# Expert selection cut into four parts and gathers called inside it, in a two-block transformer kernel

## The chip, the cores and the metric

The kernel runs on one core of a Trainium2 chip. The metric is the time of one launch on the device in microseconds; the median of three runs stands for a kernel. The engines are TensorE (PE: matmuls, with its weight loads as PEld), VectorE (DVE), ScalarE (ACT), GpSimd (POOL) and SyncE (SP). DMAs are issued from the queues of SyncE, GpSimd and ScalarE and share 16 DMA engines.

## The reference

Two transformer blocks over 256 tokens of width 1024 in float32. The first has a state-space mixer, chunked attention and a gated feed-forward layer. The second has two kinds of attention and, instead of a feed-forward layer, a mixture of very many tiny experts, which is where the change lies:

```python
q = (ht @ w_pq).reshape(T, 8, 2, 128)                    # 8 heads, two halves
sub = einsum('thpc,hpnc->thpn', q, peer_keys)            # 128 scores per head and half
s_top, i_top = top_k(sub, 16)
cand_s = s_top[:, :, 0, :, None] + s_top[:, :, 1, None, :]   # 16 x 16 pairs
best_s, pos = top_k(cand_s.reshape(T, 8, 256), 16)       # 16 of 16384 experts per head
gate = softmax(best_s)
act = gelu(einsum('cd,ckd->ck', x, peer_u[expert]))      # 128 experts per token
out = einsum('ck,ckd->cd', gate * act, peer_v[expert])
```

`peer_u` and `peer_v` have 16384 rows of 1024 each. The output is a final norm of the sum.

## The kernel before

Weights are stored as float32 tiles of 128 x 1024 (512 KB). Most matmuls use a split: ScalarE copies a tile to a high part (`whi`, L226), VectorE or, for tiles named in `POOL_LO` or flagged "P" in `specs`, GpSimd subtracts it to get the low part (`wlo`, L231), and TensorE multiplies three combinations. The order in which each engine runs its instructions is made at build time by a planner that follows the program's order where several are ready; `behind` and `chain` add a fixed order by hand. `chain` ties an instruction behind the last one tied on the same engine, as long as `self.tail` is a dictionary.

The expert layer (`peer`) works in stages. (1) Four `w_pq` tiles and, in `route`, twelve more make the queries; `scores` multiplies them with the keys. The results reach SBUF in banks of four of the sixteen head halves (`subs`). (2) `topk` selects on VectorE, first for tokens 0 to 127 (`tt` = 0), then for the others: 16 calls of `topk16` on 128 scores, three sums of candidates, 8 calls of `topk16` on 80 candidates, softmax weights with one exponential on ScalarE (L1406), and index arithmetic with one-hot products (L1434 to L1442). (3) For the first 96 tokens (`TS`) `slots` writes expert numbers and weights into `slot` with six small DMAs of GpSimd's queue (L1497); `sparse` then gathers the rows of `peer_u` with 96 indirect DMAs of 128 rows each (L1504, 512 KB), each followed by a product with accumulation on VectorE (L1509). After all 96 come 96 gathers of `peer_v`, each followed by a sum into `sacc` (L1524). Five `ug` buffers hold gathers. (4) For the other 160 tokens all 16384 experts are computed in 128 blocks: `u_chunk` for the first 44 (`U0`, L1614) and `u_mul` for the other 84 (L1631). Each block is one `peer_u` tile from SyncE's queue, 8 matmuls of TensorE (16 instructions in the trace), and a GELU of ScalarE. SyncE's tiles run ahead by 13 buffers. (5) In the second of these loops `gate_batch` makes, for 8 tokens per 4 blocks, one-hot matrices on VectorE and ScalarE, a matmul on TensorE (L1568), and the products with the gates (L1579 on ScalarE, L1581 on VectorE). (6) The last loop takes 128 blocks of `peer_v` (L1710) on TensorE for the 160 tokens, while the remaining gathers go on. Then come the output norm and the stores.

The calls `next(sparse)` say where in the program's order a gather and its product stand: in the first loop beside blocks from 26 (`S0`) on except each sixth, in the second beside 70 of 84 blocks, in the last loop beside five of six, the rest behind it. `pick` transposes the selection of each `tt` on TensorE behind block 40.

Of the kernel before, what the change touches and what calls it, by code (L numbers as in the profile page):

```python
# [21 lines left out]
D = 1024  # L22
# [110 lines left out]
class Kernel:  # L133
# [4 lines left out]
    def specs(self):  # L138
# [25 lines left out]
        for i in range(4):  # L164
            add(io["w_pq"], (i,), "LP")
        add(io["w_pq"], range(4, 16))
# [1166 lines left out]
    def topk16(self, vals, idx, src, work):  # L1333
        V = self.nc.vector
        V.max(vals[:, 0:8], src)
        V.max_index(idx[:, 0:8], vals[:, 0:8], src)
        V.match_replace(work, vals[:, 0:8], src, LOWEST)
        V.max(vals[:, 8:16], work)
        V.max_index(idx[:, 8:16], vals[:, 8:16], work)
# [34 lines left out]
    def topk(self, R, K, subs):  # L1374
        nc, V, A, G = self.nc, self.nc.vector, self.nc.scalar, self.nc.gpsimd
# [4 lines left out]
        V.tensor_copy(self.iota2, iota[:, :, None].to_broadcast([128, 128, 2]))  # L1380
        it16 = K.tile([128, 16, 16], FP16, name="it16")
        V.tensor_copy(it16, iota[:, 0:16, None].to_broadcast([128, 16, 16]))
        self.picked = []
        for tt in range(2):
            sub = subs[tt]
            vals = K.tile([128, 16, 16], F32, name="vals", bufs=2)
            idx = K.tile([128, 16, 16], U32, name="idx", bufs=2)
            for j in range(16):
                w = K.tile([128, 128], F32, name="work", bufs=2)
                self.topk16(vals[:, j], idx[:, j], sub[:, j], w)  # L1390
            cand = K.tile([128, 8, 80], F32, name="cand")
            v4 = vals.rearrange("p (h s) a -> p h s a", s=2)
            v1, v2 = v4[:, :, 0], v4[:, :, 1]
            V.tensor_tensor(cand[:, :, 0:16], v2, v1[:, :, 0:1].to_broadcast([128, 8, 16]), OP.add)
            V.tensor_tensor(cand[:, :, 16:72].rearrange("p h (a b) -> p h a b", a=7),
                            v1[:, :, 1:8, None].to_broadcast([128, 8, 7, 8]),
                            v2[:, :, None, 0:8].to_broadcast([128, 8, 7, 8]), OP.add)
            V.tensor_tensor(cand[:, :, 72:80], v1[:, :, 8:16], v2[:, :, 0:1].to_broadcast([128, 8, 8]), OP.add)
            best = K.tile([128, 8, 16], F32, name="best")
            pos = K.tile([128, 8, 16], U32, name="pos")  # L1400
            for hd in range(8):
                w = K.tile([128, 80], F32, name="work2", bufs=2)
                self.topk16(best[:, hd], pos[:, hd], cand[:, hd], w)
            e = K.tile([128, 8, 16], F32, name="gexp", bufs=2)
            V.tensor_tensor(e, best, best[:, :, 0:1].to_broadcast([128, 8, 16]), OP.subtract)
            A.activation(e, e, AF.Exp)  # L1406
            s = K.tile([128, 8], F32, name="gsum")
            V.tensor_reduce(s, e, op=OP.add, axis=AX.X)
            V.reciprocal(s, s)
            V.tensor_tensor(e, e, s[:, :, None].to_broadcast([128, 8, 16]), OP.mult)  # L1410
            id2 = K.tile([128, 2, 8, 16, 2], FP16, name="id2")
            for s_ in range(2):
                V.tensor_copy(id2[:, s_].rearrange("p h a t -> p h a t"),
                              idx.rearrange("p (h s) a -> p h s a", s=2)[:, :, s_, :, None].to_broadcast([128, 8, 16, 2]))
            sel = []
            ui = K.tile([128, 2, 128], U32, name="ui")
            uf = K.tile([128, 2, 128], F32, name="uf")
# [5 lines left out]
            ab = K.tile([128, 2, 128], F32, name="ab")  # L1423
            ab16 = K.tile([128, 2, 128], FP16, name="ab16")
            m9 = K.tile([128, 128], F32, name="m9")
# [5 lines left out]
            V.tensor_tensor(ab16[:, 1], ab[:, 1], m9, OP.subtract)  # L1431
            for s_ in range(2):
                eq = K.tile([128, 8, 16, 16], FP16, name="eq", bufs=2)
# [363 lines left out]
```

## Time and profile before

| | us |
|---|---|
| three runs: median (lowest to highest) | 1302.26 (1298.88 to 1309.69) |
| profiled execution, its own time | 1310.38 |
| its span | 1308.6 |
| TensorE busy | 1236.8 (95%) |
| VectorE busy | 896.3 (68%) |
| ScalarE busy | 494.9 (38%) |
| GpSimd busy | 464.0 (35%) |

The profile is of one execution. Times count from the start of the span; about 2 us lie outside it. The expert layer takes the second half: queries and scores up to about 690 us, the first 44 blocks to 788, the other 84 to 990, the last loop to 1292. A matmul's busy time is modelled, so a loop is best timed by the starts of its first and last instructions. "Idle before" is the time that an engine stood still ahead of an instruction, with what ended it.

### The profile page before, as it was taken

How to read it: one execution, taken by the hardware profiler on the slowest of the kernel's cores; microseconds unless marked ns; L12 is line 12 of the kernel's file. 1: busy time of each engine (PE TensorE's matmuls, PEld its weight loads, DVE VectorE, ACT ScalarE, POOL GpSimd, SP SyncE). 2: the span in 40 equal slices, each digit the busy share in tenths (PEclk: the TensorE clock that was granted, in tenths of full speed). 3: DMA queues.
4: the chain of work that ended last, by engine and by line, in shares of the span. 5: the costliest groups of instructions: out<-in, count | busy, mean ns of one | idle time of the engine just before them, and what ended most of it. 6: DMA issues, size and time to landing. Idle time of an engine off the chain costs nothing.

```text
span 1308.6 us, 22647 instructions
## 1 busy us (share of the span) xinstructions
PE 1236.8 (95%) x8650; PEld 1156.7 (88%) x8650; DVE 896.3 (68%) x1787; ACT 494.9 (38%) x1053; POOL 464.0 (35%) x400
## 2 busy tenths in 40 slices
PE   6798989998999999999899999999999999999996
PEld 5687868988979988998799999999999999888896
DVE  8996765899667888548788945777775455454433
ACT  5335655666556845645532214444440000000001
POOL 5941020665105645202300433444444333333310
PEclk9897889999999988999899999999999999999998
DMA  5322355888744737346678799999999999999991
GB/s 196 106 81 77 105 197 176 305 313 319 256 144 166 246 115 240 98 145 208 211 235 307 277 410 407 396 397 401 400 398 401 409 409 409 409 409 409 409 406 49
DMA packets 103116, 361.50 MB, mean 276 GB/s; under 512 B 15136, under 2 KB 15328, under 8 KB 102624
## 3 DMA queue, kind: packets, MB, share of 16 engines
q1 hardware_dynamic: 71904, 251.28, 52.9%
q0 software_dynamic: 30816, 108.26, 21.6%
q8 instruction: 68, 1.11, 0.3%
q10 hardware_dynamic: 288, 0.52, 0.1%
q14 instruction: 40, 0.33, 0.1%
HBM read 356.22 MB, written 2.12 MB: 274 GB/s over the span
## 4 chain that ended last, share of the span: by engine, by line
PE 51%; DMA 22%; DVE 17%; issue 4%; ACT 2%; POOL 2%; SPq 0%; DVEq 0%; POOLq 0%; ACTq 0%
DMA raw<-peer_v 17%; PE m L1631 14%; PE m L272 13%; PE acc L1710 6%; PE m L1614 4%; PE acc L858 4%; DVE wlo L231 4%; PE acc L1105 3%; DMA adaw<-w_ada 2%; PE acc L873 1%; PE g L1568 1%; POOL adaacc L410 1%; DVE adaacc L407 1%; POOL adaacc L412 1%; DMA bias<-bias 1%
## 5 line engine op out<-in xcount | busy, mean ns | idle before, releaser
L1710 PE MATMUL acc<-act,raw 128*128 128x160 f32 x2048 | 294.4, 302 | 8.3 <-DMA raw<-peer_v 1.8
L1710 PEld LDWEIGHTS acc<-act,raw 128*128 128x128 f32 x2048 | 279.8, 190 | 22.8 <-DMA raw<-peer_v 22.8
L231 DVE TENSOR_TENSOR wlo<-raw,whi 128x1024 fp32r<-128x1024 f32 x150 | 232.0, 1558 | 63.8 <-ACT whi L226 60.9
L226 ACT ACTIVATE whi<-raw 128x1024 fp32r<-128x1024 f32 x166 | 174.0, 1055 | 134.8 <-PE m L272 58.1
L1524 DVE SCALAR_TENSOR_TENSOR sacc<-ug,sw,sacc 128x1024 f32<-128x1024 f32 x94 | 120.8, 1285 | 122.3 <-DMA ug<-peer_v,slot 122.3
L1631 PE MATMUL m<-hN,raw 128*128 128x160 f32 x1344 | 187.0, 300 | 0.0
L1631 PEld LDWEIGHTS m<-hN,raw 128*128 128x128 f32 x1344 | 183.2, 190 | 0.0
L1504 POOL DMA_INDIRECT ug<-u_rows,slot x96 | 120.7, 1258 | 149.6 <-DVE act L1639 97.1
L1504 POOL DMA_INDIRECT ug<-peer_v,slot x96 | 90.5, 943 | 156.6 <-DVE sacc L1524 142.9
L1509 DVE SCALAR_TENSOR_TENSOR ug<-ug,hrow 128x1024 f32<-128x1024 f32 x96 | 116.9, 1218 | 26.9 <-DMA ug<-u_rows,slot 26.9
L272 PE MATMUL m<-h_hi,whi 128*128 128x256 f32 x768 | 117.1, 291 | 4.3 <-ACT h_hi L916 3.0
L272 PE MATMUL m<-h_hi,wlo 128*128 128x256 f32 x768 | 113.0, 286 | 5.4 <-DVE wlo L231 4.8
L272 PE MATMUL m<-h_lo,whi 128*128 128x256 f32 x768 | 116.1, 290 | 2.0 <-DVE h_lo L917 2.0
L272 PEld LDWEIGHTS m<-h_hi,whi 128*128 128x128 f32 x768 | 105.5, 196 | 8.8 <-ACT h_hi L916 3.5
L272 PEld LDWEIGHTS m<-h_hi,wlo 128*128 128x128 f32 x768 | 101.1, 192 | 7.7 <-DVE wlo L231 5.6
L272 PEld LDWEIGHTS m<-h_lo,whi 128*128 128x128 f32 x768 | 104.6, 197 | 3.3 <-DVE h_lo L917 2.4
L1718 ACT ACTIVATE fT<-acc,gt 128x160 f32<-128x160 f32 x4 | 1.6, 393 | 274.2 <-DVE fT L1720 274.0
L1614 PE MATMUL m<-hN,raw 128*128 128x160 f32 x704 | 98.2, 302 | 2.6 <-ACT act L1624 2.6
L1614 PEld LDWEIGHTS m<-hN,raw 128*128 128x128 f32 x704 | 97.5, 193 | 2.8 <-ACT act L1624 2.8
L410 POOL TENSOR_TENSOR adaacc<-adaacc,adaw 128x1024 f32<-128x1024 f32 x24 | 66.0, 2749 | 49.4 <-ACT adaw L409 48.9
L231 POOL TENSOR_TENSOR wlo<-raw,whi 128x1024 fp32r<-128x1024 f32 x16 | 39.4, 2473 | 50.3 <-ACT whi L226 44.6
L1636 ACT ACTIVATE ut<-m 128x8 f32<-128x8 f32 (+19 forms) x80 | 19.2, 240 | 99.9 <-PE m L1631 60.5
(526 smaller groups left out, 1811.9 us busy)
## 6 DMA issues: line engine op xcount, KB each, us to landing
raw<-peer_u SPq DMA_DIRECT2D x128, 512.0 KB
raw<-peer_v SPq DMA_DIRECT2D x128, 512.0 KB
raw<-w_in SPq DMA_DIRECT2D x62, 512.0 KB
adaw<-w_ada SPq DMA_DIRECT2D x48, 512.0 KB
raw<-w_gu SPq DMA_DIRECT2D x44, 512.0 KB
raw<-w_down SPq DMA_DIRECT2D x22, 512.0 KB
raw<-w_out SPq DMA_DIRECT2D x16, 512.0 KB
raw<-w_pq SPq DMA_DIRECT2D x16, 512.0 KB
```

Source lines behind the costliest of these rows:

```text
L226: i = self.nc.scalar.activation(hi, t, AF.Copy)
L231: i = e.tensor_tensor(lo, t, hi.bitcast(F32), OP.subtract)
L272: self.nc.tensor.matmul(out, w(k), x(k), start=start and c == 0, stop=stop and c == last)
L410: G.tensor_tensor(accs[1], accs[1], w, OP.add)
L858: self.nc.tensor.matmul(acc[2 * tt + n], a[:, k, tt * 128:tt * 128 + 128], w[:, 512 * n:512 * n + 512], start=first and (tt, n) not in see ...
L1105: self.nc.tensor.matmul(out, a[:, 2 * c + kk, tt * 128:tt * 128 + 128], w[:, 512 * kk:512 * kk + 512], start=c + i + kk == 0, stop=c == 3 ...
L1504: G.indirect_dma_start(t, None, rows, bass.IndirectOffsetOnAxis(self.slot[:, 0, s:s + 1].bitcast(U32), 0))
L1509: i = V.scalar_tensor_tensor(t, t, 1.0, self.hrow[g], op0=OP.mult, op1=OP.mult, accum_out=self.sdot[:, s:s + 1])
L1524: self.last = V.scalar_tensor_tensor(self.sacc[g], t, w, self.sacc[g], op0=OP.mult, op1=OP.add)
L1614: m = nc.tensor.matmul(ps, w[:, 128 * k:128 * k + 128], hN[:, k], start=k == 0, stop=k == 7)
L1631: D(nc.tensor.matmul(ps[:, 0:N], w[:, 128 * k:128 * k + 128], hN[:, k], start=k == 0, stop=k == 7))
L1710: nc.tensor.matmul(part(d), w[:, 128 * d:128 * d + 128], at(i), start=i == 0 and d % 2 == 0, stop=i == 127, skip_group_check=True)
```

## The change

- `specs`: the first four `w_pq` tiles lose the flag "P" (their low parts go from GpSimd to VectorE); tiles 8 to 15 get it (eight low parts go to GpSimd).
- `topk` becomes a generator that yields after each small piece. It works in four parts, by `tt` and half of the heads (`hf`): `first` makes the first-stage selection of some head halves, `second` the rest for four heads. All tiles of `second` are half as wide, and so there are four exponentials. The sum and the division of the softmax move behind the one-hot products. `slots` is called twice, each time for 64 of the 128 experts of a token, and issues six DMAs each time.
- Every VectorE instruction of the selection is tied (`Tied`) in the program's order; `self.tail` is a dictionary from here on, so that the products of gathered rows are tied in the same order.
- Once the first part is done, a gather is called at every third yield from yield 31 on (`EA`, `EV`): 13 of 68 yields. In the first loop they begin at block 32 instead of 26. In the second loop they stand beside three blocks of four and some more, until all 96 are done (`done`).
- `sparse` takes the `u` gathers in the order in which the halves of `slot` are written.
- In the second loop the end of a gate batch comes behind the gather and the late product of its block instead of ahead of them.

```diff
@@ specs
         for i in range(4):
-            add(io["w_pq"], (i,), "LP")
-        add(io["w_pq"], range(4, 16))
+            add(io["w_pq"], (i,), "L")
+        for i in range(4, 16):
+            add(io["w_pq"], (i,), "P" if i >= 8 else "")
@@ topk
+        class Tied:
+            def __getattr__(self, name):
+                f = getattr(nc.vector, name)
+                return lambda *a, **k: outer.chain(f(*a, **k))
+        V = Tied()
...
+        def first(tt, hf, js):
+            if (tt, hf) not in top:
+                top[tt, hf] = [K.tile([128, 8, 16], d, name=n, bufs=3) for n, d in (("vals", F32), ("idx", U32))]
+            vals, idx = top[tt, hf]
+            for j in js:
                 w = K.tile([128, 128], F32, name="work", bufs=2)
-                self.topk16(vals[:, j], idx[:, j], sub[:, j], w)
+                self.topk16(vals[:, j], idx[:, j], subs[tt][:, 8 * hf + j], w, V)
+                yield
+        def second(tt, hf):
...
+            yield
+            for hd in range(4):
                 w = K.tile([128, 80], F32, name="work2", bufs=2)
-                self.topk16(best[:, hd], pos[:, hd], cand[:, hd], w)
+                self.topk16(best[:, hd], pos[:, hd], cand[:, hd], w, V)
+                yield
+            x = K.tile([128, 4, 16], F32, name="gx", bufs=2)
+            V.tensor_tensor(x, best, best[:, :, 0:1].to_broadcast([128, 4, 16]), OP.subtract)
+            A.activation(x, x, AF.Exp)
...
+            s = K.tile([128, 4], F32, name="gsum")
+            V.tensor_reduce(s, x, op=OP.add, axis=AX.X)
+            V.reciprocal(s, s)
+            V.tensor_tensor(e, x, s[:, :, None].to_broadcast([128, 4, 16]), OP.mult)
             if tt == 0:
-                with self.tc.high_priority():
-                    self.slots(e, *sel)
+                self.slots(hf, V, e, *sel)
+            yield
+        yield from first(0, 0, range(0, 4))
+        yield from first(1, 0, range(0, 4))
+        yield from first(0, 0, range(4, 8))
+        yield from second(0, 0)
+        self.ready = True
+        yield from first(0, 1, range(0, 8))
+        yield from second(0, 1)
+        yield from first(1, 0, range(4, 8))
+        yield from second(1, 0)
+        yield from first(1, 1, range(0, 8))
+        yield from second(1, 1)
@@ slots
         for t0, n in self.TG:
+            h = n // 2
             for q in range(128 // n):
-                self.dq.dma_start(self.slot[n * q:n * q + n, :, t0:t0 + n], ids[t0:t0 + n, :, n * q:n * q + n])
+                self.dq.dma_start(self.slot[n * q:n * q + n, :, t0 + h * hf:t0 + h * hf + h],
+                                  ids[t0:t0 + n, :, h * q:h * q + h])
@@ sparse
-        for g, s in slots:
+        early = [(g, t0 + n // 2 * hf + s) for hf in range(2) for g, (t0, n) in enumerate(self.TG) for s in range(n // 2)]
+        for g, s in early:
@@ constants
-    S0 = 26
+    S0 = 32
+    EA = 31
+    EV = 3
@@ peer
-            sparse, self.tail = self.sparse(), None
+            sparse, self.tail = self.sparse(), {}
...
-                    self.topk(R, K, subs)
+                    self.ready, given = False, 0
+                    for n, _ in enumerate(self.topk(R, K, subs)):
+                        if self.ready and n >= self.EA and (n - self.EA) % self.EV == 0:
+                            next(sparse)
+                            given += 1
...
                     if c % 4 == 0:
-                        if live is not None:
-                            next(live, None)
-                            n += 8
+                        fin = live
                         live = self.gate_batch(O, pg, act, TS + 2 * c, lambda: cur[0]) if 2 * c < N else None
                     if live is not None:
                         mm = next(live)
-                    if c % 4 or c % 12 == 0:
+                    if (c % 4 != 1 or c % 8 == 1) and self.done < TS:
                         next(sparse)
                     late()
+                    if c % 4 == 0 and fin is not None:
+                        next(fin, None)
+                        n += 8
                     late = u_mul(i, n, U)
```

## Rows read from the trace of the kernel before

**Rows 1.** DMA queues, 700 to 740 us, all queues together

```profile
DMA packets 2680, 9.70 MB, mean 243 GB/s; under 512 B 375, under 2 KB 439, under 8 KB 2548
```

**Rows 2.** Table of stretches: start:end, length, busy by engine, PEclk, DMA share, GB/s

```profile
800.00:850.00 50.00, 50.00 (x414) 49.81 (x413) 34.59 (x81) 23.78 (x91) 21.62 (x17) 1.00 1.01 399
1100.00:1200.00 100.00, 94.61 (x630) 86.20 (x629) 49.14 (x39) 0.00 (x0) 36.65 (x39) 1.00 1.03 409
```

**Rows 3.** DMA queues, 1100 to 1200 us: packets, MB, share of 16 engines

```profile
q1 hardware_dynamic: 5629, 20.50, 51.2%
q0 software_dynamic: 5567, 20.27, 51.0%
```

**Rows 4.** Chain that ended last: start us, us, what (whole run)

```profile
676.79 3.00 PE m L272 x25
...
989.96 47.83 PE acc L1710 x352
...
1261.78 30.69 PE acc L1710 x224
```

**Rows 5.** DMA queues from 990 us to the end

```profile
q1 hardware_dynamic: 17266, 62.32, 49.1%
q0 software_dynamic: 15174, 55.22, 43.6%
```

**Rows 6.** TensorE in order of time: start, us, what, [idle before, releaser]

```profile
626.87 1.97 PE L367 MATMUL m<-eye,xn 128*128 128x128 f32 x8 [5.99 <-DVE xn L357]
...
737.58 43.24 PE L1614 MATMUL m<-hN,raw 128*128 128x160 f32 x304 [2.57 <-ACT act L1624]
...
796.53 1.08 PE L1568 MATMUL g<-io,jo 128*128 128x128 f16 x16
```

**Rows 7.** GpSimd in order of time, 700 to 740 us

```profile
728.75 3.31 POOL L1497 DMA_DIRECT2D slot<-ids  x6 [7.85 <-DVE best L1335]
734.27 1.04 POOL L1504 DMA_INDIRECT ug<-u_rows,slot  x1 [2.22 <-issue]
```

**Rows 8.** VectorE in order of time, 620 to 660 us

```profile
625.83 0.21 DVE L303 SCALAR_TENSOR_TENSOR rs_t<-n_r,rs_m 128x1 f32<-128x1 f32 x1
626.07 0.16 DVE L304 SCALAR_TENSOR_TENSOR n_r<-rs_t,n_r 128x1 f32<-128x1 f32 x1
...
659.10 0.87 DVE L1335 MAX8 vals<-sub 128x8 f32<-128x128 f32 x4 [1.52 <-ACT sub L1358]
```

**Rows 9.** VectorE groups, 655 to 760 us: busy, mean ns; idle before, releaser

```profile
L1509 DVE SCALAR_TENSOR_TENSOR ug<-ug,hrow 128x1024 f32<-128x1024 f32 x8 | 9.8, 1221 | 4.5 <-DMA ug<-u_rows,slot 4.5
...
L231 DVE TENSOR_TENSOR wlo<-raw,whi 128x1024 fp32r<-128x1024 f32 x7 | 8.5, 1214 | 1.6 <-ACT whi L226 1.5 <-issue 0.2
...
L1335 DVE MAX8 vals<-sub 128x8 f32<-128x128 f32 x32 | 7.1, 277 | 7.2 <-ACT sub L1358 7.2
L1437 DVE TENSOR_TENSOR eq<-eq,id 128x2048 f16<-128x2048 f16 x4 | 4.9, 1214 | 0.0
...
L1440 DVE TENSOR_TENSOR eq<-eq 128x1024 f16<-128x1024 f16 x4 | 2.7, 680 | 0.0
```

**Rows 10.** Waits of VectorE, 788 to 990 us: total, times, longest

```profile
DVE act L1581 <- ACT act L1579: 49.0, 16, 8.1
```

**Rows 11.** ScalarE in order of time, 730 to 740 us

```profile
735.60 0.31 ACT L1406 ACTIVATE gexp<-gexp 128x128 f32<-128x128 f32 x1 [5.47 <-DVE gexp L1405]
```

**Rows 12.** VectorE in order of time, 610 to 625 us

```profile
615.81 2.84 DVE L1010 TENSOR_TENSOR x<-x,gx 128x512 f32<-128x512 f32 x1
...
619.51 0.68 DVE L1010 TENSOR_TENSOR x<-x,gx 128x512 f32<-128x512 f32 x1
...
622.03 2.30 DVE L299 SCALAR_TENSOR_TENSOR rs_t<-n_r,rs_a 128x1 f32<-128x1 f32 x1
```

**Rows 13.** GpSimd in order of time, 600 to 630 us

```profile
610.90 7.20 POOL L231 TENSOR_TENSOR wlo<-raw,whi 128x1024 fp32r<-128x1024 f32 x3 [24.05 <-ACT whi L226]
621.97 2.34 POOL L231 TENSOR_TENSOR wlo<-raw,whi 128x1024 fp32r<-128x1024 f32 x1 [3.88 <-ACT whi L226]
```

More of the change, by code (lines that the diff above doesn't have):

```diff
@@ L1330, in block2, with topk16 @@
                 self.acc_tail(acc, [(mT, k) for k in range(4, 8)], False, epi, pre=self.PRE[2])
-    def topk16(self, vals, idx, src, work):
-        V = self.nc.vector
+    def topk16(self, vals, idx, src, work, V):
         V.max(vals[:, 0:8], src)
@@ L1374, in topk @@
     def topk(self, R, K, subs):
-        nc, V, A, G = self.nc, self.nc.vector, self.nc.scalar, self.nc.gpsimd
+        nc, A, D = self.nc, self.nc.scalar, self.chain
+        outer = self
+        class Tied:
[3 more added lines that the diff above has]
+        V = Tied()
         iota = R.iota
@@ L1379, in topk @@
         self.iota2 = R.pool.tile([128, 128, 2], FP16, name="iota2")
-        V.tensor_copy(self.iota2, iota[:, :, None].to_broadcast([128, 128, 2]))
+        nc.vector.tensor_copy(self.iota2, iota[:, :, None].to_broadcast([128, 128, 2]))
         it16 = K.tile([128, 16, 16], FP16, name="it16")
[L1382 to L1388, printed above, removed]
-                w = K.tile([128, 128], F32, name="work", bufs=2)
-                self.topk16(vals[:, j], idx[:, j], sub[:, j], w)
-            cand = K.tile([128, 8, 80], F32, name="cand")
+        nc.vector.tensor_copy(it16, iota[:, 0:16, None].to_broadcast([128, 16, 16]))
@@ new lines, in topk @@
+        self.picked = [[K.tile([128, 8, 16], F32, name=n, bufs=2) for n in ("gexp", "sel0", "sel1")] for _ in range(2)]
+        top = {}
+        def first(tt, hf, js):
[3 more added lines that the diff above has]
+            for j in js:
+                w = K.tile([128, 128], F32, name="work", bufs=2)
+                self.topk16(vals[:, j], idx[:, j], subs[tt][:, 8 * hf + j], w, V)
+                yield
@@ L1392, in topk @@
+        def second(tt, hf):
+            vals, idx = top.pop((tt, hf))
+            e, *sel = [a[:, 4 * hf:4 * hf + 4] for a in self.picked[tt]]
+            cand = K.tile([128, 4, 80], F32, name="cand")
             v4 = vals.rearrange("p (h s) a -> p h s a", s=2)
             v1, v2 = v4[:, :, 0], v4[:, :, 1]
-            V.tensor_tensor(cand[:, :, 0:16], v2, v1[:, :, 0:1].to_broadcast([128, 8, 16]), OP.add)
+            V.tensor_tensor(cand[:, :, 0:16], v2, v1[:, :, 0:1].to_broadcast([128, 4, 16]), OP.add)
@@ L1415, in topk @@
-            sel = []
-            ui = K.tile([128, 2, 128], U32, name="ui")
-            uf = K.tile([128, 2, 128], F32, name="uf")
+                            v1[:, :, 1:8, None].to_broadcast([128, 4, 7, 8]),
+                            v2[:, :, None, 0:8].to_broadcast([128, 4, 7, 8]), OP.add)
+            V.tensor_tensor(cand[:, :, 72:80], v1[:, :, 8:16], v2[:, :, 0:1].to_broadcast([128, 4, 8]), OP.add)
+            best = K.tile([128, 4, 16], F32, name="best")
+            pos = K.tile([128, 4, 16], U32, name="pos")
@@ L1418, in topk @@
+            ui = K.tile([128, 2, 64], U32, name="ui")
+            uf = K.tile([128, 2, 64], F32, name="uf")
             pf = pos.rearrange("p h k -> p (h k)")
@@ L1487, in rows_init, with slots @@
         self.sdot, self.sw = [SP.tile([128, TS], F32, name=n) for n in ("sdot", "sw")]
-    def slots(self, e, i, j):
-        nc, V, TS = self.nc, self.nc.vector, self.TS
+    def slots(self, hf, V, e, i, j):
+        TS = self.TS
         fl = lambda t: t.rearrange("p h k -> p (h k)")
-        ids = self.SP.tile([128, 2, 128], F32, name="ids")
+        ids = self.SP.tile([128, 2, 64], F32, name="ids", bufs=2)
         V.scalar_tensor_tensor(ids[0:TS, 0].bitcast(U32), fl(i)[0:TS], 128.0, fl(j)[0:TS], op0=OP.mult, op1=OP.add)
@@ L1512, in sparse @@
                 self.chain(i)
+            self.done += 1
             yield
@@ L1536 @@
     U0 = 44
-    S0 = 26
+    S0 = 32
+    EA = 31
+    EV = 3
     U1 = 126
+    done = 0
     UT = 4
```

40 lines of the change are left out of this document (13 added, 27 removed).

## Prediction

> **What bounds the kernel now.** The page's first part names TensorE as the busiest engine by far, so a gain has to come from TensorE's own gaps; the other views say what makes them. The DMA queues from 700 to 740 us come first: the DMA engines move only 243 GB/s there [rows 1]. In the table of stretches they move 399 GB/s in the expert-score loop and 409 GB/s in the last loop, which I take as full; TensorE is busy throughout the one and not in the other [rows 2].
>
> The queues from 1100 to 1200 us show how the last loop shares the DMA: SyncE's queue, which brings `peer_v` blocks to TensorE, moves 20.50 MB, and GpSimd's, which brings gathered rows, 20.27 MB [rows 3]. A block and a gather are both 512 KB (0.524 MB), so each queue delivers 39 in 100 us, one in 2.56 us. TensorE needs less: in the chain that ended last, 47.83 us for 352 instructions, 16 to a block, is 2.17 us a block [rows 4]. So while gathers run, TensorE's lead shrinks by 0.39 us a block, and then it waits. Once they are over, the last 14 blocks (224 instructions) run at TensorE's own rate, in 30.69 us [rows 4].
>
> This makes a model of the last loop. From 989.96 us GpSimd's queue still moves 55.22 MB, or 105.3 gathers, and SyncE's 62.32 MB, of which 0.52 is output: 117.9 blocks, so 10.1 of the 128 had landed before [rows 4, 5]. The gathers end at 990 + 105.3 x 2.56 = 1259.6 us (the chain says 1261.78) and TensorE 14 x 2.17 us later, near 1290 (1292.47 by the chain). So the end is the start of the loop, plus 0.39 us for each gather left, plus 2.17 us for each block not yet landed. The start of the loop is set by TensorE alone, whose larger gaps ahead of it are 5.99 us at 626.87 and 2.57 us at 737.58 [rows 6].
>
> **The change, part by part.**
>
> *Gathers moved forward.* Before, 15 `u` gathers are called beside the first 44 blocks and 70 beside the other 84: 85 of 96 ahead of the last loop. After, the selection calls 13 (at yields 31, 34, ... 67 of 68), the first loop 10 (blocks 32 to 43 without 36 and 42) and the second 73: all 96. The last loop loses 11; as perhaps one `v` gather is under way at its start, I count 105.3 - 95 = 10.3, at 0.39 us **-4.0 us**. That holds if the lead of 10.1 blocks is kept, which asks for DMA room elsewhere. The room: from 700 to 740 us 40 x (409 - 243)/409 = 16 us are unused, 12 gathers at 1.28 us [rows 1, 2]. Now the slots are written from 728.75 and the first gather starts at 734.27 [rows 7]. In the second loop the load becomes (84 + 73)/(84 + 70) x 399 = 407 GB/s, just under 409. Bounds: no block of the lead lost (0), or three (+6.5); I take +1.
>
> *Selection in four tied parts.* Untied, independent instructions overlap: four MAX8 of 277 ns take 0.87 us, a step of 0.20 [rows 8, 9]. A dependent one starts 0.03 us after its predecessor's end (625.83 + 0.21, then 626.07) [rows 8]. A tied `topk16` has three dependent pairs (max to index, replace to max, max to index), each 0.11 us dearer: 48 calls x 3 x 0.11 = 16 us of VectorE. Halving adds fixed costs: a product of 1024 elements takes 680 ns, not half of 1214 [rows 9]; over the instructions that now come four times instead of twice I estimate 14 us. 13 row products at 1.22 us are 16 us [rows 9]. Between 655 and 760 us VectorE has 105 us, less 13.3 idle, 9.8 of row products and 8.5 of low parts: 73 of selection [rows 9]. It becomes 73 + 16 + 14 + 16 = 119 us, from 659.10 [rows 8] less 3 (below) to 775. Its first quarter (12 calls of 1.50 us, 4 of 1.25, 9 of the rest, all estimates from these rows) is done near 690, and gathers can start near 697, 37 us sooner. VectorE's time costs nothing while it is covered: the transposes of `pick` stand behind block 40, near 780. Covered by 5 us; past that, each late microsecond costs one. I take 0.
>
> Apart from the sum: the Trainium skill, "VectorE: DVE Perf Modes", section "The DRAIN you can't avoid", says that the next operation waits until the pipe has emptied, semaphore or not. By that the tie would be free, the selection would end near 759, the gate wait below would fall away and the sum be 2 us lower. The step of 0.20 us between MAX8 of 277 ns [rows 8, 9] speaks against it.
>
> *Ten rows called in the first loop.* Row 14 and on follow the selection on VectorE: five are there at 775, the others come at 2.56 us each, number 23 near 790, the second loop's first near 794. The gate columns are tied behind that one, and TensorE reaches the first gate matmul at 796.53 [rows 6]: a wait of 0 to 6 us, I take **+2**. After that 3.5 gathers per four blocks fit the shared rate.
>
> *Gating one place later.* In the second loop VectorE stands 49.0 us, in 16 waits, at the head of its queue for ScalarE's half of the gating (L1581) [rows 10], with a row product and the next gate columns behind it. These now go first. TensorE has no gap there, so 0; it helps the gathers keep to 407 GB/s.
>
> *Four exponentials for two.* ScalarE stands at each until VectorE delivers. At the second it now waits 5.47 us [rows 11], and TensorE loses 2.57 us [rows 6], so about 2.9 us of waiting are covered by the PSUM buffers. After: from a gain of 2.6 (all covered) to four waits that lose 2.7 each (+8). Between these ends I take +0.5, a loss a little larger than the present one.
>
> *Low parts.* The first four `w_pq` tiles go from GpSimd to VectorE. On GpSimd they stand in the way: its run 610.90 to 618.10 covers VectorE's L1010, 2.84 us against 0.68, and the one at 621.97 covers L299, 2.30 us against 0.21 for L303 of the same width [rows 8, 12, 13]. Both lie ahead of the 5.99 us gap. Removed: 2.16 + 2.09 = 4.2 us. VectorE then does the four in 1.21 us each [rows 9], three of them at best in its idle time ahead of 615. From -4.2 to +0.6 (all four in the way), I take **-2.7**. Tiles 8 to 15 go to GpSimd at 2.34 us [rows 13], less than TensorE takes for one (25 matmuls in 3.00 us) [rows 4]; hidden by this they cost 0, unhidden at most 8 x 1.1 = 9. As they are nearly hidden, I take +0.7.
>
> **Sum.** -4.0 + 1 + 0 + 2 + 0 + 0.5 - 2.7 + 0.7 = -2.5 us. Against the profiled execution's own 1310.38 this is 1307.9. The runs shown have a median of 1302.26, 8.1 lower; the same 2.5 off gives 1299.8, or **1300 us**.
>
> **The rivals.**
> 1. *About even*, the sum: 1294 to 1310 us. 0.63.
> 2. *All cover holds and the lead grows*: gathers fill the unused 16 us, the lead reaches the 13 buffers of the loop (2.9 x 2.17 = -6.3), ScalarE's gap closes (-2.6), the low parts give 4.2: -4.0 - 6.3 - 2.6 - 4.2 = -17, or 1285 us. For it: the unused DMA time [rows 1]. Against: 407 of 409 GB/s leaves little for the lead to grow on. 0.14.
> 3. *ScalarE waits in its order* (slower): the selection, 46 us longer, brings its exponentials later than ScalarE's queue has them, and ScalarE blocks the GELU that empties TensorE's banks. It decides from 2.9 us of waiting at each; at 7.1 us, four times, it costs 4 x 4.2 = 17 and with the other terms 1316 us. For it: one of two does this now [rows 11]. Against: some 8 us of VectorE work (by the estimates above) lie between an exponential's input and the first use of its output, so VectorE itself isn't held. 0.15.
> 4. *The tie does not bring gathers forward*: if the first quarter ends after 728 us, the DMA room stays empty and the 11 gathers eat into the lead. The second loop has 10/409 x 190 = 4.6 us of room, 4 gathers; 7 blocks are lost, 7 x 2.17 = 15; with -4.0 and the rest (+0.5) 1314 us. It needs the quarter 38 us later than reckoned. 0.08.
>
> **How the numbers follow.** The predicted time is case 1's. To leave out no more than 2 in 10 the range reaches into both sides and takes in the bounds on the gate wait and the lead: 1287 to 1317 us. Faster by over 1% (about what a measurement of this kernel can tell from no change) is below 1289: nearly all of case 2, 0.13. Slower by over 1% is above 1315: most of case 3, some of case 4 and of case 1's tail, 0.17. The rest, 0.70, is within 1%.
>
> **What would show it.** Right: a first `u` gather near 697 us; all 96 ahead of TensorE's last loop and some 50 MB left in GpSimd's queue from there; about 10 blocks landed at its start; the gap ahead of L367 near 3 us; the selection's end near 775. Wrong: gaps over 3 us at L1614 (case 3); a first gate matmul more than 12 us after the loop's start; fewer than 8 blocks landed; a first gather after 728 us (case 4).

## The result, and the profile after

The changed kernel takes **1313.2 us** (median of 6 runs, 1310.0 to 1315.7) beside 1304.9 for the kernel before in the same comparison (6 runs, 1298.9 to 1309.7): a ratio of 1.0061 with a 95% interval of 1.0038 to 1.0084, so it is 5 to 11 us slower. I had said 1300 us, a gain of 2.5. The profiled execution of the changed kernel took 1310.93 us, with a span of 1309.1.

Line numbers of after lie one higher up to the routing code (L273, L368) and some 30 higher behind it: the first loop is L1646, the second L1663, the first gate matmul L1600, a row product L1537, the last loop L1747; everything tied in the selection stands at L1381.

**TensorE.** First its waits from 560 to 1000 us in the kernel after (engine, line, what it waited for: total us, times, longest), then the four lines in order of time in which the largest one stands (start, us, instruction, idle before it).

```profile
PE g L1600 <- DVE io L1596: 10.9, 1, 10.9
PE m L368 <- DVE xn L358: 3.0, 1, 3.0
PE m L1663 <- ACT act L1670: 1.8, 1, 1.8
```

```profile
784.86 3.48 PE L1663 MATMUL m<-hN,raw 128*128 128x160 f32 x16 [1.84 <-ACT act L1670]
799.20 1.89 PE L1600 MATMUL g<-io,jo 128*128 128x128 f16 x16 [10.86 <-DVE io L1596]
800.88 10.03 PE L1663 MATMUL m<-hN,raw 128*128 128x160 f32 x64
810.75 1.08 PE L1600 MATMUL g<-io,jo 128*128 128x128 f16 x16
```

The two gaps of before [rows 6] have shrunk: 5.99 us ahead of the transposes is now 3.0, and the 2.57 us at the exponential is gone. In their place stand two that before did not have. TensorE waits 1.84 us for a GELU of ScalarE, which itself has waited 6.98 us for VectorE to finish its copies of the gates (L1484 to L1486). Then TensorE is done with its blocks at 788.34 and waits 10.9 us for the first gate columns.

```profile
784.50 0.30 ACT L1670 ACTIVATE act<-m 128x160 f32<-128x160 f32 x1 [6.98 <-DVE g L1486]
```

**VectorE**, in order of time, is what it waits for: the end of the selection, the last row product ahead of the columns, and the columns `jo` and `io`.

```profile
774.36 0.23 DVE L1381 TENSOR_TENSOR gexp<-gx,gsum 128x64 f32<-128x64 f32 x1
...
795.55 1.23 DVE L1537 SCALAR_TENSOR_TENSOR ug<-ug,hrow 128x1024 f32<-128x1024 f32 x1 [0.75 <-DMA ug<-u_rows,slot]
796.70 0.69 DVE L1593 TENSOR_TENSOR jo<-iota,jb 128x1024 f16<-128x1024 f16 x1
...
798.45 0.69 DVE L1596 TENSOR_TENSOR io<-eq,g 128x1024 f16<-128x1024 f16 x1
```

**The last loop** starts at 994.35 us. Its queues from there on (packets, MB, share of 16 engines; the window runs to 1400 us, past the end of the span, so these shares can't be held against those of [rows 5]), and its last link in the chain that ended last (start, us):

```profile
q1 hardware_dynamic: 17249, 62.27, 38.5%
q0 software_dynamic: 13701, 49.86, 30.9%
```

```profile
1240.37 52.43 PE acc L1747 x384
```

49.86 MB are 95 gathers, against 105.3 before [rows 5]; 62.27 MB less 0.52 of output are 117.8 blocks, so 10.2 had landed. The loop ends at 1292.63, after 298.3 us (before: from 989.79 to 1292.31, 302.5).

**A common zero.** Profiled executions of kernels that differ only behind 600 us reach the start of the first `acc<-whi,mT` group anywhere between 582 and 594 us: 594.27 before, 590.08 after. So I compare traces from that landmark on. Then the first gate matmul stands at 202.3 us before and 209.1 after, the last loop starts at 395.5 and 404.3, and it ends at 698.0 and 702.5. The profiled pair is 4.5 us apart from the landmark to that end, just under the lower end of what the medians say (5 to 11). The balance below explains these 4.5; the rest is not seen in this pair. How well such traces agree is shown by kernels whose code is the same up to the last loop: it starts at 404.3 and 406.4 us (after, after_pace), 397.6 and 393.8 (untied, untied_pace), 395.5 and 396.0 (before, before_pace).

### The profile page after: what moved, and what is told of

It reads as the page before. It is cut to its first block, busy times and chain, and to the rows that moved or that the text cites. A ratio compares the mean times of both kernels' runs of the same rounds, so it can differ in the third digit from the quotient of the medians.

```text
span 1309.1 us, 22702 instructions
## 1 busy us (share of the span) xinstructions
PE 1230.9 (94%) x8649; PEld 1154.4 (88%) x8650; DVE 921.1 (70%) x1845; ACT 499.3 (38%) x1058; POOL 467.9 (36%) x410
## 4 chain that ended last, share of the span: by engine, by line
PE 47%; DMA 20%; DVE 19%; issue 6%; POOL 4%; ACT 2%; SPq 0%; POOLq 0%; ACTq 0%; DVEq 0%
DMA raw<-peer_v 14%; PE m L1663 13%; PE m L273 11%; PE acc L1747 9%; PE acc L859 4%; DVE wlo L232 4%; PE acc L1106 3%; DMA adaw<-w_ada 2%; DVE idx L1381 2%; PE g L1600 1%; DVE vals L1381 1%; POOL adaacc L411 1%; DVE ug L1537 1%; PE acc L874 1%; DVE eq L1381 1%
## 5 line engine op out<-in xcount | busy, mean ns | idle before, releaser
L1747 PE MATMUL acc<-act,raw 128*128 128x160 f32 x2048 | 291.8, 302 | 6.7 <-DMA raw<-peer_v 1.0
L1747 PEld LDWEIGHTS acc<-act,raw 128*128 128x128 f32 x2048 | 279.6, 190 | 18.8 <-DMA raw<-peer_v 18.7
L232 DVE TENSOR_TENSOR wlo<-raw,whi 128x1024 fp32r<-128x1024 f32 x146 | 224.4, 1549 | 59.4 <-ACT whi L227 58.0
L1663 PE MATMUL m<-hN,raw 128*128 128x160 f32 x1344 | 189.6, 302 | 1.8 <-ACT act L1670 1.8
L1663 PEld LDWEIGHTS m<-hN,raw 128*128 128x128 f32 x1344 | 185.3, 192 | 2.1 <-ACT act L1670 2.1
L1531 POOL DMA_INDIRECT ug<-u_rows,slot x96 | 110.2, 1148 | 167.9 <-DVE ug L1537 87.9
L1537 DVE SCALAR_TENSOR_TENSOR ug<-ug,hrow 128x1024 f32<-128x1024 f32 x96 | 116.5, 1218 | 7.2 <-DMA ug<-u_rows,slot 7.1
L273 PE MATMUL m<-h_hi,whi 128*128 128x256 f32 x768 | 115.5, 289 | 4.1 <-ACT h_hi L917 2.9
L273 PE MATMUL m<-h_hi,wlo 128*128 128x256 f32 x768 | 113.7, 287 | 5.2 <-DVE wlo L232 4.6
L273 PE MATMUL m<-h_lo,whi 128*128 128x256 f32 x768 | 114.2, 287 | 2.0 <-DVE h_lo L918 2.0
L273 PEld LDWEIGHTS m<-h_hi,whi 128*128 128x128 f32 x768 | 104.3, 194 | 8.1 <-ACT h_hi L917 3.5
L273 PEld LDWEIGHTS m<-h_hi,wlo 128*128 128x128 f32 x768 | 101.4, 192 | 7.5 <-DVE wlo L232 5.5
L273 PEld LDWEIGHTS m<-h_lo,whi 128*128 128x128 f32 x768 | 102.7, 194 | 3.1 <-DVE h_lo L918 2.4
L1646 PE MATMUL m<-hN,raw 128*128 128x160 f32 x704 | 96.1, 299 | 0.0
L1646 PEld LDWEIGHTS m<-hN,raw 128*128 128x128 f32 x704 | 95.7, 190 | 0.0
L232 POOL TENSOR_TENSOR wlo<-raw,whi 128x1024 fp32r<-128x1024 f32 x20 | 49.0, 2458 | 29.5 <-ACT whi L227 20.9
```

Of the source, the lines that this page charges most:

```text
L232: i = e.tensor_tensor(lo, t, hi.bitcast(F32), OP.subtract)
L273: self.nc.tensor.matmul(out, w(k), x(k), start=start and c == 0, stop=stop and c == last)
L1531: G.indirect_dma_start(t, None, rows, bass.IndirectOffsetOnAxis(self.slot[:, 0, s:s + 1].bitcast(U32), 0))
L1537: i = V.scalar_tensor_tensor(t, t, 1.0, self.hrow[g], op0=OP.mult, op1=OP.mult, accum_out=self.sdot[:, s:s + 1])
L1646: m = nc.tensor.matmul(ps, w[:, 128 * k:128 * k + 128], hN[:, k], start=k == 0, stop=k == 7)
L1663: D(nc.tensor.matmul(ps[:, 0:N], w[:, 128 * k:128 * k + 128], hN[:, k], start=k == 0, stop=k == 7))
```

## The experiments

All are timed in five rounds beside the kernel before, whose median was 1305.5, 1303.7 and 1304.6 us in the three groups. "After" is 1313.2. Times in the last four columns come from TensorE in order of time (gathers left: from GpSimd's queue), from the landmark on. The ratio is an estimate from the runs themselves and can differ by 0.2% from that of the two medians.

| kernel | median us | ratio to before | first gate | last loop starts | gathers left | its length |
|---|---|---|---|---|---|---|
| before | 1304.9 | 1 | 202.3 | 395.5 | 105 | 302.5 |
| after | 1313.2 | 1.0061 (1.0038 to 1.0084) | 209.1 | 404.3 | 95 | 298.3 |
| flags_only | 1300.7 | 0.9965 (0.9941 to 0.9989) | 199.2 | 392.5 | 106 | 304.4 |
| fin_only | 1304.5 | 0.9976 (0.9955 to 0.9998) | 202.4 | 395.6 | 105 | 302.5 |
| untied | 1300.8 | 0.9966 (0.9941 to 0.9990) | 204.3 | 397.6 | 95 | 298.8 |
| gate_free | 1309.8 | 1.0028 (1.0001 to 1.0055) | 204.9 | 398.2 | 99.5 | 303.5 |
| sel_no_rows | 1308.8 | 1.0032 (1.0014 to 1.0050) | 200.8 | 394.1 | 108 | 303.9 |
| few_rows | 1305.4 | 1.0023 (1.0002 to 1.0045) | 199.4 | 394.1 | 100 | 300.4 |
| old_flags | 1317.9 | 1.0101 (1.0080 to 1.0122) | 216.4 | 412.1 | 95 | 298.7 |
| before_pace | 1292.0 | 0.9913 (0.9890 to 0.9937) | 202.8 | 396.0 | 105 | 291.9 |
| after_pace | 1292.7 | 0.9916 (0.9885 to 0.9947) | 210.8 | 406.4 | 95 | 278.2 |
| untied_pace | 1280.2 | 0.9824 (0.9804 to 0.9845) | 200.5 | 393.8 | 95 | 278.2 |

**One part alone: the prefetch marks.** The kernel before with the new marks of `w_pq`.

```diff
-            add(io["w_pq"], (i,), "LP")
-        add(io["w_pq"], range(4, 16))
+            add(io["w_pq"], (i,), "L")
+        for i in range(4, 16):
+            add(io["w_pq"], (i,), "P" if i >= 8 else "")
```

> The kernel before with only the flags of the w_pq tiles changed. Theory A (GpSimd's low parts hold up VectorE's two-input operations ahead of the queries): TensorE's gap ahead of L367 falls from 6.0 to 3 us and the whole kernel gains 3 us, 1302 us. Theory B (the gain is taken back by low parts on GpSimd that TensorE waits for, or by a later wait): within 1 us of before, 1304 to 1306 us.

Measured: 4.6 us faster, and the gap ahead of the transposes is what the prediction made of it.

```profile
PE m L368 <- DVE xn L358: 3.2, 1, 3.2
PE m L1615 <- ACT act L1625: 2.6, 1, 2.6
```

The last loop starts 3.0 us earlier than in before, as the -2.7 has it. It lasts 1.9 us longer, so the traces end 1.1 us apart, where the medians have 4.6 (1.4 to 7.7 by the interval). TensorE waits nowhere for the eight low parts on GpSimd; what they cost VectorE stands below. The loss is in the other parts.

**One part alone: gating one place later.**

```diff
-                        if live is not None:
-                            next(live, None)
-                            n += 8
+                        fin = live
...
+                    if c % 4 == 0 and fin is not None:
+                        next(fin, None)
+                        n += 8
```

> The kernel before with only the end of a gate batch moved behind the gather and the late product. Theory A (VectorE's 49 us of standing at L1581 are off the path): VectorE's wait for ScalarE falls below 25 us, and the time stays within 1.5 us of before. Theory B (these waits thin the gathers' DMA out, 399 instead of 409 GB/s, and the lead of peer_v blocks with it): 3 to 5 us faster than before.

Measured: 1.0 us by the medians, up to 6 by the interval, and the landmarks of before to 0.1 us. Zero is what the trace supports; a gain of a few us isn't excluded by the times. VectorE's wait for ScalarE at L1581 fell to 23.2 us, as A has it, but 30.2 us are now waited at the next such product (L1639): the wait has moved.

**The tie taken out of after.**

```diff
-        V = Tied()
+        V = nc.vector
```

> The changed kernel with the VectorE instructions of the selection left to the planner's order; only the row products stay tied to each other. Theory A (the tie makes each topk16 0.33 us dearer and so the selection 16 us longer): the selection ends 10 to 16 us earlier, near 762 us, the wait at the first gate matmul falls below 4 us, and the time is 6 to 10 us below the changed kernel. Theory B (the late gathers and not the length of the selection make the wait): the wait stays above 7 us and the time within 3 us of the changed kernel.

Measured: 12.5 us below after, more than A's 6 to 10, to the level of the marks alone. VectorE's last selection line is this, and TensorE reaches the first gate without a wait:

```profile
749.77 0.22 DVE L1453 TENSOR_TENSOR sel<-eq 128x64 f32<-128x64 f16 x1
```

```profile
790.70 1.08 PE L1600 MATMUL g<-io,jo 128*128 128x128 f16 x16
```

The selection ends 163.6 us after the landmark, 184.5 in after. But two exponentials now hold TensorE, in the form that before had once:

```profile
PE m L1646 <- ACT act L1656: 5.0, 2, 2.7
```

So the tie has a use, it keeps ScalarE's order; and the eleven gathers taken out of the last loop (5.6 us of its length against flags_only) are paid for ahead of it, by these 5 us. In untied_pace, whose code is the same up to the last loop, the two gaps are 3.7 us together and the last loop starts at 393.8, so how much is paid is known only as 1 to 5 us.

**No row products inside the tied selection.** `EA = 31` becomes 1000; 13 gathers move to the last loop.

> The changed kernel with no gather or row product inside the tied selection: its 13 rows move to the last loop, and nothing else changes. Theory A (the tie itself is the cost: 1.57 us for a top-16 in place of 1.17): the selection ends near 760 us, VectorE makes the ten rows of the first loop at once, the wait at the first gate falls from 10.9 to between 0 and 4 us, and the start of the last loop comes 8 to 10 us earlier after the landmark; the last loop has some 108 gathers and lasts about 5 us longer (13 times 0.39 us), so the time is some 4 us below the changed kernel, about 1309. Rival C (the row products inside the selection are free on VectorE, as they fill the gaps that the tie leaves): the selection still ends near 770, the wait at the first gate stays at 8 us or more, and with the longer last loop the time is that of the changed kernel or 3 us above it.

Measured: 4.4 us below after, as A has it. The selection ends at 758.2 us, 14.6 earlier from the landmark (13 products of 1.22 us are 15.9), and the gate has no wait:

```profile
757.97 0.23 DVE L1381 TENSOR_TENSOR gexp<-gx,gsum 128x64 f32<-128x64 f32 x1
```

```profile
789.11 1.08 PE L1600 MATMUL g<-io,jo 128*128 128x128 f16 x16
```

TensorE waits once, 3.7 us, for the copies behind the transposed selection. The last loop starts 10.2 us earlier and lasts 5.6 longer. So the tie alone does not make the gate late, nor do the 13 rows alone: the sum of them does.

**Five gathers in place of ten beside the first loop.** `S0 = 32` becomes 38; the tie and the 13 rows stay. This is the step of the prediction that I suspected, by itself.

> The changed kernel with five gathers called beside the first loop (blocks 38 to 43 without 42) in place of ten; the tie and the 13 rows inside the selection stay, and five gathers move to the last loop. Theory A (the step of the prediction that failed is the ten rows of the first loop: the gate columns are tied behind row 24, whose data come at 795.6 us): the columns stand behind row 19, whose data come near 783, so the wait at the first gate falls from 10.9 to between 0 and 2 us, the last loop starts 8 to 11 us earlier after the landmark, has 100 gathers and lasts 2 us longer; the time is 1305 to 1308. Rival B (the columns are held up anyway, by the rows that the second loop calls ahead of them, or the lead of the last loop pays): 1310 or more.

Measured: 7.8 us below after by the medians, some 5 by the ratios. The columns stand behind row 19, and TensorE's wait is nearly gone:

```profile
777.32 1.23 DVE L1537 SCALAR_TENSOR_TENSOR ug<-ug,hrow 128x1024 f32<-128x1024 f32 x1 [1.22 <-DMA ug<-u_rows,slot]
...
778.47 0.69 DVE L1593 TENSOR_TENSOR jo<-iota,jb 128x1024 f16<-128x1024 f16 x1
```

```profile
781.78 1.89 PE L1600 MATMUL g<-io,jo 128*128 128x128 f16 x16 [1.78 <-DVE io L1596]
```

The last loop starts 10.2 us earlier and lasts 2.1 us longer, for five gathers more: 0.4 us a gather, the price in the prediction. A holds.

**No gathers called in the second loop's first four blocks**, another way to let the columns pass.

```diff
-                    if (c % 4 != 1 or c % 8 == 1) and self.done < TS:
+                    if c >= 4 and (c % 4 != 1 or c % 8 == 1) and self.done < TS:
```

> The changed kernel, but no gather is called beside the first four blocks of the second loop (4 of the 96 u gathers move into the last loop). Theory A (the first gate columns stand behind row products 24 to 26 on VectorE, and TensorE stands 10.9 us at the first gate matmul, after which it also runs slower for about 2 us): the wait falls below 3 us, the last loop starts 8 to 12 us earlier, costs 4 x 0.39 = 1.6 us more, and the time is 7 to 10 us below the changed kernel (about 1304 us, level with before). Theory B (the DMA can't bring the gathers in time wherever they stand): the wait only moves to the second gate batch, and the time stays within 3 us of the changed kernel (1310 to 1316 us).

Measured: 3.4 us below after, between the two. The wait at the gate is gone, but TensorE waits 5.3 us just ahead of it for ScalarE's half of the work (1.8 in after); the other two lie ahead of the selection.

```profile
PE m L1663 <- ACT act L1670: 5.3, 1, 5.3
PE m L368 <- DVE xn L358: 4.2, 1, 4.2
PE m L273 <- DVE qT L1632: 2.9, 1, 2.9
```

The last loop starts 6.1 us earlier, with 4.5 more gathers left and a lead of 9.3 blocks in place of 10.2, and lasts 5.2 us longer. A stall was removed, and most of it came back as gathers and lead. In this execution the two gaps ahead of the selection are 4.1 us longer than in after, and the selection ends 3.6 us later (188.1 against 184.5), so what the edit gives by itself is not clear from this trace. few_rows removes it more cheaply, as it lets the second loop call from its start.

**After with the old marks**, to see whether what TensorE saves ahead of the gate is just waited away there.

```diff
-            add(io["w_pq"], (i,), "L")
-        for i in range(4, 16):
-            add(io["w_pq"], (i,), "P" if i >= 8 else "")
+            add(io["w_pq"], (i,), "LP")
+        add(io["w_pq"], range(4, 16))
```

> The changed kernel with the old prefetch marks of the query weights put back, and everything else as changed. On the kernel before, the new marks alone gained 4.6 us (the stall ahead of the first transposes went from 6.0 to 3.2 us and a later one went). Theory A (what TensorE saves ahead of the first gate is lost again in the wait for that gate, because VectorE with its tied selection arrives last; the two are a maximum): the changed kernel without the new marks is no slower than with them, within 2.5 us of 1311 to 1313, its wait at the first gate being some 4 to 5 us shorter (about 6 us). Theory B (the terms add): it is 4 to 5 us slower, 1316 to 1318, the wait at the first gate unchanged at 11 us.

Measured: 4.6 us slower than after. That is B's time, but not by B's road, and A's time is wrong:

```profile
PE m L1662 <- ACT act L1669: 10.6, 1, 10.6
PE m L367 <- DVE xn L357: 6.5, 1, 6.5
PE g L1599 <- DVE io L1595: 4.9, 1, 4.9
```

The wait at the gate did fall to 4.9 us, only because 10.6 us are waited just ahead of it, for the same late selection through ScalarE (its copies for the transposed selection wait, and the GELU that empties TensorE's bank stands behind them). VectorE is later too: with the old marks it makes twelve low parts between 620 and 690 us, with the new ones four.

```profile
L231 DVE TENSOR_TENSOR wlo<-raw,whi 128x1024 fp32r<-128x1024 f32 x12 | 14.5, 1218 | 3.1 <-ACT whi L226 2.4 <-PE m L272 0.6
```

Eight more at 1.22 us are 9.8 us, five of them inside the selection; it starts 1.5 us later from the landmark and ends 9.2 us later (193.7 against 184.5), and the gate comes 7.3 later. So I had taken the two arrivals as independent, and they aren't: the marks set VectorE's as well. What stays of theory A is that the later arrival counts, and here it is VectorE's.

**The last loop, paced.** The model of the last loop said that gathers, taking half of the DMA whether or not they are urgent, end early and leave TensorE behind. So let a gather wait for TensorE:

```diff
+                ms.append(m)
+                self.pace = ms[i - self.PL] if i >= self.PL else None
-                if i % 6:
+                if i % 4:
                     next(sparse, None)
...
-            t = fetch(self.io["peer_v"].rearrange("a b c -> (a b) c"), s)
+            t = fetch(self.io["peer_v"].rearrange("a b c -> (a b) c"), s, self.pace)
```

Here `fetch` makes the gather depend on that matmul, PL is 4, and `before_pace` keeps `i % 6`.

> The changed kernel without the tie (1300.8 us), and in the last loop the gather issued at block i waits until TensorE is done with block i - 4, three gathers to four blocks. Now the gathers and the weights share the queues half and half, 95 gathers are through at about block 104, TensorE waits some 20 us for weights by then, and nothing but weights moves afterwards. Theory A (that split is what the last loop loses): paced, 118 blocks and 95 gathers of 0.524 MB at 409 GB/s need 273 us and TensorE 278 us, so the loop lasts 280 to 288 us in place of 298.8, and the time is 1283 to 1291. Rival B (the loop is bound by the bytes and by gather latency, not by the order): 295 us or more, within 4 us of 1300.8.

> The kernel before with only this change: in the last loop the gather of a second-table row issued at block i waits until TensorE is done with block i - 4, five gathers to six blocks as before. 105 gathers and 118 blocks of 0.524 MB at 409 GB/s need 286 us and TensorE 278 us. Theory A: the last loop lasts 287 to 294 us in place of 302.5, and the time is 1294 to 1300 where the kernel before takes 1305. Rival B (order of the bytes does not matter): within 3 us of the kernel before. If both paced kernels follow A, the eight to ten gathers fewer in the last loop of the changed kernel are worth what the bytes cost, some 10 us, where without pacing they were worth 4.

> The changed kernel, tie and all, with the last loop paced (a gather issued at block i waits until TensorE is done with block i - 4, three to four blocks). Pacing gained 20.6 us on the untied kernel by its last loop alone (298.8 to 280.1 us). Theory A (the two are separate: the tie costs ahead of the first gate, the split of the queues costs in the last loop): the last loop lasts 279 to 282 us, the wait at the first gate stays near 11 us, and the time is 1292 to 1295, some 12 us above the untied paced kernel at 1280. Rival B (a later start of the last loop finds more blocks landed, so that the paced loop takes back part of the tie's cost): 1282 to 1289.

Measured: 1280.2, 1292.0 and 1292.7 us, with last loops of 278.2, 291.9 and 278.2 us. A holds in all three, though the first two are 2 to 3 us faster than it said, and untied_pace is faster than both kernels, by 23 us than before. (The 280.1 us in the text on after_pace is 2 too many.) In before_pace only the waiting is new; in the other two the gathers' spacing changes too (`i % 4`), and what that gives by itself was not tried. Table of stretches with the columns of [rows 2], from 1200 to 1250 us, of the kernel before and of untied_pace:

```profile
1200.00:1250.00 50.00, 47.65 (x313) 42.82 (x313) 24.85 (x20) 0.00 (x0) 18.49 (x20) 1.00 1.03 409
```

```profile
1200.00:1250.00 50.00, 50.00 (x370) 50.00 (x370) 21.85 (x17) 0.00 (x0) 19.10 (x18) 1.00 1.03 407
```

The DMA moves as much in both, but TensorE gets through 370 instructions where it had 313. With 95 gathers the loop is bound by TensorE (128 blocks of 2.17 us are 278); with 105 it isn't quite (291.9). The tie costs the same 12.5 us with pacing as without (1292.7 against 1280.2), so the two are separate. Of this pair the traces show it all: the last loop starts 12.6 us apart (406.4 and 393.8) and is equally long.

## Why the prediction was wrong

**The step that failed** is "Ten rows called in the first loop", +2 (0 to 6). It measured a wait of 10.9 us, and a slow start behind it. Three things make it up, from the landmark on:
- The wait that I reckoned: 2 us.
- TensorE arrives earlier than before: ready for the gate at 198.3 us in place of 202.3, 4.0 us. These are the 3.0 us won ahead of the transposes and the 2.6 us of the exponential, less the 1.8 us gap that is new; the sum of these is 3.8. I had set VectorE's 794 us against TensorE's old 796.53, and in other lines of the same sum had booked TensorE's own savings. A meeting of two engines is the later of two times; what the earlier one saves only makes it wait longer.
- VectorE arrives later: its `io` ends at 799.14 us, or 209.1 from the landmark, where I had 204.3 (798.5 in the time of before). 4.8 us. The selection ended 3.8 us later than reckoned from the landmark (at 774.6 in the trace, 775 predicted, but the whole first half ran 4.2 us earlier in that execution): it started 1.7 us later (63.5 us from the landmark, 61.8 reckoned) and took 121.0 us in place of 119. The rest is the rows' own time.

Together 10.8 us. few_rows, which takes only five rows from ahead of the columns, removes 9.1 of the 10.9, which shows that this queue is the cause; untied and sel_no_rows shorten it in other places and remove it all.

The clock comes on top. Stretches of after, columns as before:

```profile
785.00:788.00 3.00, 3.00 (x16) 2.93 (x16) 1.23 (x2) 2.51 (x10) 1.84 (x2) 0.68 1.04 425
788.00:799.00 11.00, 0.33 (x2) 0.00 (x0) 8.38 (x14) 0.30 (x1) 7.14 (x5) 0.50 1.01 389
799.00:803.00 4.00, 3.81 (x24) 3.81 (x25) 4.00 (x7) 0.70 (x1) 3.23 (x3) 0.50 0.88 269
803.00:808.00 5.00, 5.00 (x38) 5.00 (x37) 4.41 (x11) 2.95 (x12) 2.81 (x3) 0.98 0.86 280
```

The granted clock had fallen before the wait (0.68 in the stretch behind the 1.84 us gap) and is 0.50 (1.2 GHz) through the wait and in the stretch behind it. So the first gate's 16 matmuls take 1.89 us against 1.08 for the next, and the 64 behind them 10.03 us against 8.91 where the clock is full: 1.9 us that I had not priced. It is not the price of a long wait alone: in few_rows, behind gaps of 1.98 and 1.78 us, the same two take 1.89 and 9.57 us. Before had such a loss too, behind its 2.57 us gap (304 matmuls in 43.24 us [rows 6], some 2.0 us over the 2.17 us a block), and after has one behind the 1.84 us gap (16 in 3.48 us, 1.3 over). These two nearly cancel, and the balance leaves them out.

The balance to the start of the last loop: -3.0 - 2.6 + 1.8 + 10.9 + 1.9 = +9.0; measured +8.8. The last loop gives back 4.2. Hence +4.6, measured +4.5.

**The other steps.**
- *Gathers out of the last loop, -4.0:* right. 95.1 gathers left (95 predicted), 10.2 blocks landed (10), 4.2 us shorter. +1 for a lost lead was too much: the lead held.
- *Selection's length:* 119 us predicted, to 775; the trace says 121.0 and 774.6. That it came so near is luck. With row products (1.22 us each) and idle time taken out, I estimate from the traces 74 us in flags_only (92.0 with 5 products and 11.8 idle), 80 in untied (halves, no tie: 99.3 with 15 products and 1.5 idle) and 106 in sel_no_rows (no products) and after: halving costs some 6 us, not 14, and the tie some 27, not 16. The first gather came at 694.10 (697 predicted). But "0" was its price only for the transposes of `pick`; its length came back through the rows and the gate columns. The halves, the tie and the 13 rows fill the slack that VectorE had; taking the 13 rows, five later rows or the tie out of it brings the time down each time.
- *DMA room ahead of 740 us:* right in place, wrong in what it bought. The queues move 356 GB/s from 690 to 740 us in after, but the next 50 us fall to 336, in which before moved 400: VectorE, busy with the selection, frees no gather buffers (when the selection ends, five gathered rows lie ready, and their products run from 774.50 on without a wait). Rows 14 and on then wait for data, 21 us from the selection's end to the last of them, where I had 15 to 19.

```profile
690.00:740.00 50.00, 50.00 (x370) 50.00 (x370) 46.97 (x216) 12.53 (x29) 15.05 (x19) 1.00 0.95 356
740.00:790.00 50.00, 46.49 (x334) 45.84 (x332) 42.83 (x164) 12.09 (x36) 15.55 (x14) 0.96 0.95 336
```

- *Gating one place later, 0:* right. VectorE's wait at the head of its queue for ScalarE's half, 49.0 us in 16 [rows 10], is 16.6 in 19, with 25.8 us in 49 waits now at the next product, and time did not follow (fin_only).

```profile
DVE act L1671 <- ACT ut L1668: 25.8, 49, 1.8
DVE act L1613 <- ACT act L1611: 16.6, 19, 1.2
```

- *Exponentials, +0.5:* in after none holds TensorE, so -2.6, which the gate then waits away; untied shows two at 2.7 and 2.3 us, so rival 3's mechanism exists at this size only, and the tie keeps it off.
- *Low parts, -2.7 + 0.7:* right in place (the gap ahead of the transposes is 3.0, "near 3" predicted). Missed: the marks also set when the selection ends, 9.2 us earlier than with the old ones, as old_flags shows. And GpSimd's eight are not free for VectorE: a copy just ahead of the selection, 0.28 us in before, takes 7.57 in after, as long as GpSimd's run of low parts beside it. ScalarE has copied the first scores by 651.36 us, and the selection's first instruction comes at 653.62. In gate_free, where the copy runs ahead of GpSimd's, it takes 0.29 us, but the scores come later there. It is the effect by which I had priced L1010; I had counted it for the old low parts and not for the new ones.

```profile
655.43 0.28 DVE L1380 CAST iota<-iota 128x256 f16<-128x256 f32 x1
```

```profile
645.93 7.57 DVE L1387 CAST iota<-iota 128x256 f16<-128x256 f32 x1 [1.87 <-DMA iota<-consts]
...
653.62 0.28 DVE L1381 MAX8 vals<-sub 128x8 f32<-128x128 f32 x1
```

```profile
646.26 7.08 POOL L232 TENSOR_TENSOR wlo<-raw,whi 128x1024 fp32r<-128x1024 f32 x3
```

- *The tie's price*, 16 us of VectorE by [rows 8, 9], was right in kind and too low, by the estimate above. A tied `topk16` takes 1.57 us on 128 scores (MAX8 of consecutive calls at 655.20 and 656.77) and 1.31 on 80 candidates (675.77 and 677.08), where I had 1.50 and 1.25, and the index arithmetic, which is tied too, I had not counted. By the Trainium skill's rule ("VectorE: DVE Perf Modes", "The DRAIN you can't avoid"), which would have made the tie free, untied would not have gained 12.5 us.
- *Rivals:* 2 had two of its gains (the exponential's gap, the low parts), not the growing lead; 3 and 4 did not happen. None had the mechanism that decided, though the sign given for it, a first gate matmul over 12 us after the loop's start, was there (776.00 to 799.20).

**Open.** The medians put untied 12.5 us below after (8 to 17 by the intervals), their traces only 6.1 from the landmark on. The paired kernels with pacing show the whole 12.6, so the 6.1 may be this execution's; that was not tried. The part ahead of the landmark scatters by 12 us from one profiled execution to the next, also where the code is the same up to the last loop (594.3 us before, 585.4 in before_pace). The record shows what the scatter goes with: over the 35 runs of before in the first group (1296.56 to 1312.88 us) the longer runs tend to have the lower mean granted clock (0.977 at the shortest, 0.965 at the longest; correlation -0.81). Why the clock differs stays open. Nor was it tried whether fewer rows, no tie and pacing together go below 1280.

## What to carry to other kernels

Where a change frees the waiting engine and lengthens the queue of the one that it waits for, put both arrivals on one time line and take the later; don't add a saving of the first to a wait estimated on the old line. A row product, a tie or a column is cheap on a half-idle engine until its queue holds something that the bound engine will ask for: count the queue up to that instruction, not the engine's busy share. And where a hidden stream shares the DMA with the stream that feeds the bound engine, tie its issues to that engine's progress: here a change of a few lines gave 0.9% on before, and 1.8% together with the parts of the change that hold.

## What the runs showed of the hardware

- The two queues shared the DMA half and half though only one of their readers was urgent: 20.5 and 20.3 MB in 100 us [rows 3], with TensorE waiting on one of them. Paced, the total stayed at 407 to 409 GB/s, and only the share moved (23.0 and 17.8 MB in the same 100 us of untied_pace).
- The granted clock was 0.50 while TensorE waited 10.9 us, and 0.50 in the stretch from 799 to 803 us behind it. It had fallen ahead of that wait, behind a gap of 1.84 us. In few_rows, behind gaps of 1.98 and 1.78 us, the first gate took 1.89 us too.
- A tied `topk16` on VectorE steps by 1.57 us though its instructions are the same: the MAX8 of untied work run in pairs of 0.47 us, those of tied work take 0.28 and 0.29 each with the next one behind its end.
- A run of GpSimd's low parts and a VectorE copy beside it: the copy took 7.57 us in after (GpSimd's run 7.08), 0.28 in before and 0.29 in gate_free, where GpSimd's run stands elsewhere.
